# Conditioning's scale and shift on two engines, x normed on GpSimd and transposed early

## The chip, the cores and the metric

One Trainium2 chip, one of its cores. The metric is device time in microseconds of one execution of the whole program; the time before is the median of three runs, 3528.78 us.

## The reference

Two transformer blocks run one behind the other on x (512 tokens by 1024 features, float32), each with two layers of a mixer and a feed-forward part. What the change touches is the very beginning of the first block: a conditioning vector c gives a scale and a shift for each feature, x is normed over its features, scaled and shifted, and goes into the first projection of the first mixer.

```python
cond = jax.nn.silu(c)
mod = cond @ w_ada[layer] + b_ada[layer]            # 1024 -> 6 * 1024
sh1, sc1, g1, sh2, sc2, g2 = jnp.split(mod[:, None, :], 6, axis=-1)
h = rms_norm(x, norm_mix[layer]) * (1.0 + sc1) + sh1
proj = h @ w_in                                     # gated_deltanet_mixer, layer 0
```

## The kernel before

The program is written in Python loops that are fully unrolled; a planner then lays out each engine's queue by program order and by when it believes inputs to be ready, and each engine runs its queue in that order. Tiles are 128 partitions high. x lies in four tiles of 128 tokens by 1024 features, and the products want it turned: `h` is eight pairs of tiles (high part and low part, which together make up a float32) of 128 features by 512 tokens. Each product is three matmuls (`mm3`, lines 109 to 114): high by high, high weights by low h, low weights by high h. Weights come in through three raw buffers (`raw`), are split on ScalarE (line 88) and VectorE (line 89) into high and low parts, with three buffers each (`whi`, `wlo`).

`opening` (lines 179 to 208) works in two halves of four feature tiles, k0 = 0 and 4. Ahead of both, ScalarE squares x and sums it up by token; VectorE, then GpSimd (lines 84 and 85) make the inverse root `rs` for two token tiles at a time. For each half, the scale (i = 1) and then the shift (i = 0): two loads of 1 MB of `w_ada` (line 192), eight VectorE operations that multiply a slab of 128x512 by the conditioning's column and add it up into `acc` (lines 196 and 198), and `mod_cols` (lines 445 to 459), where four TensorE matmuls against a column of ones sum `acc` over partitions and VectorE adds the bias. In the first half four weight tiles are asked for next (`gdn_w_ab`, then the key, value and query tiles of head 0). `turned` (lines 141 to 166) norms x on VectorE into a raw buffer (line 146), transposes it on TensorE (line 151), applies scale and shift out of PSUM on VectorE (line 165) or ScalarE (line 163), and splits the result. Then come the products, bank by bank: four banks with four feature tiles each, 48 matmuls in each half, 96 in all. The banks' results are taken by `gdn`, which copies the first (line 545) and runs a convolution on each of the others (lines 602 and 603), and goes on with head 1's three projections.

Later in the program the same conditioning work is done in the background (`mod`, lines 423 to 443), one raw buffer at a time; its scale and shift go through `mod_cols` as well, eight matmuls each.

Of the kernel before, what the change touches and what calls it, by code (L numbers as in the profile page):

```python
# [9 lines left out]
F32 = mybir.dt.float32  # L10
F32R = mybir.dt.float32r
AF = mybir.ActivationFunctionType
ALU = mybir.AluOpType
# [3 lines left out]
P = 128  # L17
S = 512
D = 1024
NT = S // P  # L20
KD = D // P
# [9 lines left out]
class Net:  # L31
# [146 lines left out]

    def opening(self, pool, aps):

        nc = self.nc
        self.load_x()
        self.new_h()
        rs = [self.inverse_rms(u) for u in range(2)]
        ws, banks = [], [self.mm_bank() for _ in aps]
        for k0 in (0, 4):
            for i in (1, 0):
                n0 = i * D + k0 * P
                acc = pool.tile([P, 512], F32, name=self.nm("acc"))
                for c in range(2):  # L190
                    w = pool.tile([P, 4, 512], F32, name=self.nm("ada"))
                    nc.sync.dma_start(w, self.a["w_ada"][0, c * 512:(c + 1) * 512, n0:n0 + 512].rearrange("(k p) n -> p k n", p=P))
                    for k in range(4):
                        g = self.cond[:, 4 * c + k:4 * c + k + 1]
                        if c + k == 0:
                            nc.vector.tensor_scalar(acc, w[:, k, :], g, None, ALU.mult)
                        else:
                            nc.vector.scalar_tensor_tensor(acc, w[:, k, :], g, acc, ALU.mult, ALU.add)
                self.mod_cols(0, i, acc, k0, 4)
            if k0 == 0:  # L200
                ws = [self.weights(ap) for ap in aps]
            for u in range(2):
                self.turned(u, rs[u], k0, self.mods[0, 1], self.mods[0, 0])
            for (whi, wlo), bank in zip(ws, banks):
                for k in range(k0, k0 + 4):
                    s = slice(k * P, (k + 1) * P)
                    self.mm3(bank, (whi[:, s], wlo[:, s]), self.hk(k), k == 0, k == KD - 1)
        self.ready = banks
# [234 lines left out]
        return [lambda k=k: step(k) for k in range(KD)]  # L443

    def mod_cols(self, l, i, acc, j0, n):
        nc = self.nc
        if j0 == 0:
            self.mods[l, i] = self.mp.tile([P, KD], F32, tag=f"mod{i}", name=self.nm("mod"), bufs=2)
        o = self.mods[l, i][:, j0:j0 + n]
        b = self.mp.tile([P, KD], F32, tag="mb", name=self.nm("mb"), bufs=2)  # L450
        nc.sync.dma_start(b, self.a["b_ada_col"][l * 6 + i])
        pt = self.aux()
        for j in range(n):
            nc.tensor.matmul(pt[:, j:j + 1], acc[:, j * P:(j + 1) * P], self.ones[:, 0:1], start=True, stop=True)  # L454
        nc.vector.tensor_tensor(o, pt[:, :n], b[:, j0:j0 + n], ALU.add)
        if i % 3 == 1:
            g = self.mp.tile([P, KD], F32, tag="mg", name=self.nm("mg"), bufs=2)
            nc.sync.dma_start(g, self.a["norm_mix" if i == 1 else "norm_ffn"][l])
            nc.vector.scalar_tensor_tensor(o, o, 1.0, g[:, j0:j0 + n], ALU.add, ALU.mult)
# [1368 lines left out]
```

## Time and profile before

| | |
|---|---|
| runs | 3527.29, 3528.78, 3529.30 us; median 3528.78 |
| profiled execution | 3530.39 us; its span 3528.6 us |
| TensorE busy | 3444.9 us, 98% |
| VectorE busy | 2134.6 us, 60% |
| ScalarE busy | 1413.1 us, 40% |
| GpSimd busy | 175.0 us, 5% |

PE is TensorE's matmuls, PEld its weight loads, DVE is VectorE, ACT ScalarE, POOL GpSimd, SP the engine that issues the loads. The span runs from the first instruction of the profiled execution to its last, and times in the trace count from its start. Records of float32 matmuls come in pairs: one matmul of line 454 is two records. Matmuls are pipelined, so a record's duration is longer than the distance to the next record's start; the distance is what a matmul costs in a dense stretch.

### The profile page before, as it was taken

The numbers are of one execution on the slowest core, as the hardware profiler recorded it, in microseconds if no ns is written. First come the engines' busy times: TensorE is split into PE (matmuls) and PEld (weight loads), VectorE is DVE, ScalarE is ACT, GpSimd is POOL, SyncE is SP. The second block draws the span as 40 slices with busy tenths as digits, with TensorE's granted clock in tenths as the row PEclk, the third lists the DMA queues.
The fourth block names the chain that finished last, engine by engine and source line by source line (L and its number), as shares of the span: only waits on it lengthen the run. The fifth ranks groups of instructions, "written<-read, shape, count | busy, mean of one in ns | idle before, by whom it ended". The sixth has DMA issues, their size and how long they took to land.

```text
span 3528.6 us, 54339 instructions
## 1 busy us (share of the span) xinstructions
PE 3444.9 (98%) x21522; PEld 2992.9 (85%) x21522; DVE 2134.6 (60%) x3835; ACT 1413.1 (40%) x2867; POOL 175.0 (5%) x300
## 2 busy tenths in 40 slices
PE   6999999999999999999999999999999999999998
PEld 5888898989998889897777789898977778898988
DVE  7766675554455734349966645536489776456364
ACT  4444442223455422233445434434334544344342
POOL 0211100000211000000000000000000000000000
PEclk9999999999999999999999999999999999999999
DMA  6322145542332322244322232333353322233332
GB/s 218 96 90 78 41 140 188 185 147 87 110 103 78 118 93 95 93 150 138 93 84 73 72 119 92 94 99 99 115 159 90 96 70 72 83 119 101 97 97 78
DMA packets 137279, 374.68 MB, mean 106 GB/s; under 512 B 24480, under 2 KB 33392, under 8 KB 137024
## 3 DMA queue, kind: packets, MB, share of 16 engines
q1 hardware_dynamic: 137024, 371.20, 33.5%
q8 instruction: 170, 2.79, 0.3%
q14 instruction: 85, 0.70, 0.1%
HBM read 347.45 MB, written 8.48 MB: 101 GB/s over the span
## 4 chain that ended last, share of the span: by engine, by line
PE 89%; DVE 6%; ACT 2%; issue 1%; POOL 1%; DMA 0%; SPq 0%; DVEq 0%; POOLq 0%; ACTq 0%
PE mm L112 25%; PE mm L113 25%; PE mm L114 25%; PE aux L619 2%; PE mm L1459 2%; PE aux L1428 2%; DVE cy L1243 1%; PE aux L1450 1%; PE aux L608 1%; DVE wlo L89 1%; PE aux L151 1%; PE aux L952 1%; PE aux L454 1%; ACT aux L133 0%; PE mm L985 0%
## 5 line engine op out<-in xcount | busy, mean ns | idle before, releaser
L112 PE MATMUL mm<-hhi,whi 128*128 128x512 f32 (+1 forms) x2776 | 1057.5, 382 | 8.1 <-ACT hhi L88 6.4
L114 PE MATMUL mm<-hhi,wlo 128*128 128x512 f32 (+1 forms) x2776 | 1048.6, 378 | 4.1 <-DVE wlo L89 4.1
L113 PE MATMUL mm<-hlo,whi 128*128 128x512 f32 (+1 forms) x2776 | 1049.5, 379 | 0.0
L89 DVE TENSOR_TENSOR wlo<-raw,whi 128x1024 fp32r<-128x1024 f32 (+3 forms) x523 | 595.4, 1139 | 602.2 <-ACT whi L88 595.0
L88 ACT CAST whi<-raw 128x1024 fp32r<-128x1024 f32 (+3 forms) x523 | 512.7, 981 | 1046.0 <-PE mm L113 485.6
L112 PEld LDWEIGHTS mm<-hhi,whi 128*128 128x128 f32 x2776 | 524.5, 189 | 103.0 <-ACT hhi L88 7.2
L114 PEld LDWEIGHTS mm<-hhi,wlo 128*128 128x128 f32 x2776 | 524.8, 189 | 100.6 <-DVE wlo L89 5.2
L113 PEld LDWEIGHTS mm<-hlo,whi 128*128 128x128 f32 x2776 | 525.2, 189 | 93.3 <-issue 2.0
L112 PE MATMUL mm<-whi,hidhi 128*128 128x256 f32 x1056 | 297.2, 281 | 0.0
L114 PE MATMUL mm<-whi,hidlo 128*128 128x256 f32 x1056 | 297.1, 281 | 0.0
L113 PE MATMUL mm<-wlo,hidhi 128*128 128x256 f32 x1056 | 297.1, 281 | 0.0
L112 PE MATMUL mm<-whi,hhi 128*128 128x256 f32 (+1 forms) x736 | 216.0, 293 | 1.5 <-ACT whi L88 1.5
L114 PE MATMUL mm<-whi,hlo 128*128 128x256 f32 (+1 forms) x736 | 213.4, 290 | 0.0
L113 PE MATMUL mm<-wlo,hhi 128*128 128x256 f32 (+1 forms) x736 | 213.3, 290 | 0.0
L113 PEld LDWEIGHTS mm<-wlo,hidhi 128*128 128x128 f32 x1056 | 200.6, 190 | 0.3
L112 PEld LDWEIGHTS mm<-whi,hidhi 128*128 128x128 f32 x1056 | 200.6, 190 | 0.3
L114 PEld LDWEIGHTS mm<-whi,hidlo 128*128 128x128 f32 x1056 | 200.6, 190 | 0.0
L1243 DVE SCALAR_TENSOR_TENSOR cy<-cc,cw,cy 128x497 f32<-128x497 f32 (+19 forms) x240 | 177.0, 747 | 9.1 <-ACT cy L1240 5.3
L112 PEld LDWEIGHTS mm<-whi,hhi 128*128 128x128 f32 x736 | 140.8, 191 | 3.0 <-ACT whi L88 1.9
L113 PEld LDWEIGHTS mm<-wlo,hhi 128*128 128x128 f32 x736 | 140.8, 191 | 0.5 <-DVE wlo L89 0.2
L114 PEld LDWEIGHTS mm<-whi,hlo 128*128 128x128 f32 x736 | 140.8, 191 | 0.5 <-DVE hlo L89 0.2
L436 DVE SCALAR_TENSOR_TENSOR macc<-raw,cond,macc 128x1024 f32<-128x1024 f32 x70 | 89.8, 1283 | 76.9 <-DMA raw<-in_w_ada_dram 76.6
(383 smaller groups left out, 5261.1 us busy)
## 6 DMA issues: line engine op xcount, KB each, us to landing
raw<-in_w_ffn_in_dram SPq DMA_DIRECT2D x88, 512.0 KB, 3.6
raw<-in_ffn_w_up_dram SPq DMA_DIRECT2D x88, 512.0 KB, 3.6
raw<-in_w_ada_dram SPq DMA_DIRECT2D x80, 512.0 KB, 3.9
raw<-in_w_gate_dram SPq DMA_DIRECT2D x64, 512.0 KB, 3.6
raw<-in_w_in_dram SPq DMA_DIRECT2D x50, 512.0 KB, 3.5
raw<-in_gdn_w_in_dram SPq DMA_DIRECT2D x32, 512.0 KB, 3.8
raw<-in_w_ffn_out_dram SPq DMA_DIRECT2D x32, 512.0 KB, 3.6
raw<-in_w_branch_dram SPq DMA_DIRECT2D x64, 256.0 KB, 2.6
```

Source lines behind the costliest of these rows:

```text
L88: self.nc.scalar.copy(hi, src)
L89: self.nc.vector.tensor_tensor(lo, src, hi.bitcast(F32), ALU.subtract)
L112: mm(out, ahi, bhi, start=first, stop=False)
L113: mm(out, ahi, blo, start=False, stop=False)
L114: mm(out, alo, bhi, start=False, stop=last)
L151: nc.tensor.transpose(pt[:, i * 256 + v * P:i * 256 + (v + 1) * P], xn[:, v, (j + i) * P:(j + i + 1) * P], self.ident)
L436: nc.vector.scalar_tensor_tensor(acc[0], raw, self.cond[:, k:k + 1], acc[0], ALU.mult, ALU.add)
L454: nc.tensor.matmul(pt[:, j:j + 1], acc[:, j * P:(j + 1) * P], self.ones[:, 0:1], start=True, stop=True)
L619: T_.matmul(bank[:, sl[n]], l[:, sl[n]], r[:, sl[n]], start=True, stop=True)
L1243: taps.append(lambda d=d: stt(y[:, d:], c[:, :S - d], cw[:, f, 30 - d:31 - d], y[:, d:], ALU.mult, ALU.add))
L1428: T_.matmul(pt, qs[g][:, sl[i]], k[g][:, k0:k0 + w], start=b == 0, stop=b == 1)
L1459: T_.matmul(po[halves[g], sl[i]], v, p, start=b == 0 and coarse is not None, stop=last and b == len(todo) - 1)
```

## The change

In `opening` the loads of scale and shift of a half are issued one behind the other (`columns`). The scale is added up on VectorE as before. The shift is no longer: each of its eight 128x512 slabs becomes the stationary operand of four TensorE matmuls with the conditioning's column as the moving one, which accumulate in one PSUM bank; `mod_take`, split off from `mod_cols`, adds the bias. x is normed on GpSimd (`turn`) into buffers of its own, transposed, and copied by ScalarE to `xt`, ahead of scale and shift. These are then applied by feature tile over all 512 tokens: ScalarE makes the high part, VectorE the whole value in place and the low part. The fourth weight tile is split into buffers of its own. The products run feature tile by feature tile, the banks inside.

```diff
@@ -178,31 +178,65 @@
 
     def opening(self, pool, aps):
 
+
         nc = self.nc
         self.load_x()
         self.new_h()
         rs = [self.inverse_rms(u) for u in range(2)]
-        ws, banks = [], [self.mm_bank() for _ in aps]
+        banks = [self.mm_bank() for _ in aps]
+        xt = pool.tile([P, KD, S], F32, name="xt")
+
+        def columns(k0, i):
+
+            n0 = i * D + k0 * P
+            ws = []
+            for c in range(2):
+                w = pool.tile([P, 4, 512], F32, name=self.nm("ada"))
+                nc.sync.dma_start(w, self.a["w_ada"][0, c * 512:(c + 1) * 512, n0:n0 + 512].rearrange("(k p) n -> p k n", p=P))
+                ws += [w[:, k, :] for k in range(4)]
+            return ws
+
+        def turn(k0, u):
+            xn = pool.tile([P, 2, 512], F32, tag="xn", name=self.nm("xn"), bufs=2)
+            for v in range(2):
+                nc.gpsimd.tensor_scalar(xn[:, v, :], self.x[2 * u + v][:, k0 * P:(k0 + 4) * P], rs[u][:, v:v + 1], None, ALU.mult)
+            for j in (0, 2):
+                pt = self.aux()
+                for i in range(2):
+                    for v in range(2):
+                        nc.tensor.transpose(pt[:, i * 256 + v * P:i * 256 + (v + 1) * P],
+                                            xn[:, v, (j + i) * P:(j + i + 1) * P], self.ident)
+                nc.scalar.copy(xt[:, k0 + j:k0 + j + 2, u * 256:(u + 1) * 256], pt.rearrange("p (i c) -> p i c", i=2))
+
+        ws = []
         for k0 in (0, 4):
-            for i in (1, 0):
-                n0 = i * D + k0 * P
-                acc = pool.tile([P, 512], F32, name=self.nm("acc"))
-                for c in range(2):
-                    w = pool.tile([P, 4, 512], F32, name=self.nm("ada"))
-                    nc.sync.dma_start(w, self.a["w_ada"][0, c * 512:(c + 1) * 512, n0:n0 + 512].rearrange("(k p) n -> p k n", p=P))
-                    for k in range(4):
-                        g = self.cond[:, 4 * c + k:4 * c + k + 1]
-                        if c + k == 0:
-                            nc.vector.tensor_scalar(acc, w[:, k, :], g, None, ALU.mult)
-                        else:
-                            nc.vector.scalar_tensor_tensor(acc, w[:, k, :], g, acc, ALU.mult, ALU.add)
-                self.mod_cols(0, i, acc, k0, 4)
+            scale, shift = columns(k0, 1), columns(k0, 0)
+            acc = pool.tile([P, 512], F32, name=self.nm("acc"))
+            for k, w in enumerate(scale):
+                g = self.cond[:, k:k + 1]
+                if k == 0:
+                    nc.vector.tensor_scalar(acc, w, g, None, ALU.mult)
+                else:
+                    nc.vector.scalar_tensor_tensor(acc, w, g, acc, ALU.mult, ALU.add)
+            for u in range(2):
+                turn(k0, u)
+            self.mod_cols(0, 1, acc, k0, 4)
             if k0 == 0:
-                ws = [self.weights(ap) for ap in aps]
-            for u in range(2):
-                self.turned(u, rs[u], k0, self.mods[0, 1], self.mods[0, 0])
-            for (whi, wlo), bank in zip(ws, banks):
-                for k in range(k0, k0 + 4):
+                ws = [self.weights(ap, pool if i == 3 else None) for i, ap in enumerate(aps)]
+            pt = self.aux()
+            for k, w in enumerate(shift):
+                for j in range(4):
+                    nc.tensor.matmul(pt[:, j:j + 1], w[:, j * P:(j + 1) * P], self.cond[:, k:k + 1],
+                                     start=k + j == 0, stop=k == KD - 1 and j == 3)
+            self.mod_take(0, 0, pt, k0, 4)
+            gain, shift = self.mods[0, 1], self.mods[0, 0]
+            for k in range(k0, k0 + 4):
+                hi, lo = self.hk(k)
+                nc.scalar.activation(hi, xt[:, k, :], AF.Identity, bias=shift[:, k:k + 1], scale=gain[:, k:k + 1])
+                nc.vector.tensor_scalar(xt[:, k, :], xt[:, k, :], gain[:, k:k + 1], shift[:, k:k + 1], ALU.mult, ALU.add)
+                nc.vector.tensor_tensor(lo, xt[:, k, :], hi.bitcast(F32), ALU.subtract)
+            for k in range(k0, k0 + 4):
+                for (whi, wlo), bank in zip(ws, banks):
                     s = slice(k * P, (k + 1) * P)
                     self.mm3(bank, (whi[:, s], wlo[:, s]), self.hk(k), k == 0, k == KD - 1)
         self.ready = banks
@@ -443,15 +477,18 @@
         return [lambda k=k: step(k) for k in range(KD)]
 
     def mod_cols(self, l, i, acc, j0, n):
+        pt = self.aux()
+        for j in range(n):
+            self.nc.tensor.matmul(pt[:, j:j + 1], acc[:, j * P:(j + 1) * P], self.ones[:, 0:1], start=True, stop=True)
+        self.mod_take(l, i, pt, j0, n)
+
+    def mod_take(self, l, i, pt, j0, n):
         nc = self.nc
         if j0 == 0:
             self.mods[l, i] = self.mp.tile([P, KD], F32, tag=f"mod{i}", name=self.nm("mod"), bufs=2)
         o = self.mods[l, i][:, j0:j0 + n]
         b = self.mp.tile([P, KD], F32, tag="mb", name=self.nm("mb"), bufs=2)
         nc.sync.dma_start(b, self.a["b_ada_col"][l * 6 + i])
-        pt = self.aux()
-        for j in range(n):
-            nc.tensor.matmul(pt[:, j:j + 1], acc[:, j * P:(j + 1) * P], self.ones[:, 0:1], start=True, stop=True)
         nc.vector.tensor_tensor(o, pt[:, :n], b[:, j0:j0 + n], ALU.add)
         if i % 3 == 1:
             g = self.mp.tile([P, KD], F32, tag="mg", name=self.nm("mg"), bufs=2)
```

## Rows read from the trace of the kernel before

**Rows 1.** The page: busy time by engine; the chain that ended last, by engine.

```profile
PE 3444.9 (98%) x21522; PEld 2992.9 (85%) x21522; DVE 2134.6 (60%) x3835; ACT 1413.1 (40%) x2867; POOL 175.0 (5%) x300
...
PE 89%; DVE 6%; ACT 2%; issue 1%; POOL 1%; DMA 0%; SPq 0%; DVEq 0%; POOLq 0%; ACTq 0%
```

**Rows 2.** Table by stretch, opening: length, busy time by engine, clock, DMA.

```profile
11.80:38.30 26.50, 7.51 (x32) 6.81 (x32) 23.11 (x39) 6.13 (x11) 0.70 (x1) 1.00 0.92 350
...
49.30:55.80 6.50, 3.65 (x33) 3.40 (x31) 3.57 (x11) 3.08 (x8) 0.00 (x0) 1.00 0.40 101
```

**Rows 3.** Timeline of VectorE, opening: start, time, line, operation, count, idle before.

```profile
11.81 0.49 DVE L196 TENSOR_SCALAR acc<-ada,cond 128x512 f32<-128x512 f32 x1 [0.38 <-DMA ada<-in_w_ada_dram]
12.34 5.47 DVE L198 SCALAR_TENSOR_TENSOR acc<-ada,cond,acc 128x512 f32<-128x512 f32 x7
19.83 0.16 DVE L455 TENSOR_TENSOR mod<-aux,mb 128x4 f32<-128x4 f32 x1 [2.02 <-PE aux L454]
...
20.11 0.48 DVE L196 TENSOR_SCALAR acc<-ada,cond 128x512 f32<-128x512 f32 x1
...
30.41 1.67 DVE L146 TENSOR_SCALAR raw<-x,rs 128x512 f32<-128x512 f32 x4
```

**Rows 4.** Timeline of TensorE, opening.

```profile
17.96 1.83 PE L454 MATMUL aux<-ones,acc 128*128 128x1 f32 x8 [17.96 <-DVE acc L198]
...
31.00 3.81 PE L151 MATMUL aux<-ident,raw 128*128 128x128 f32 x16 [2.98 <-issue]
38.32 0.80 PE L112 MATMUL mm<-hhi,whi 128*128 128x512 f32 x1 [3.51 <-ACT hhi L88]
...
43.30 0.63 PE L114 MATMUL mm<-hhi,wlo 128*128 128x512 f32 x1
43.73 0.48 PE L112 MATMUL mm<-hhi,whi 128*128 128x512 f32 x1
...
49.30 1.84 PE L454 MATMUL aux<-ones,acc 128*128 128x1 f32 x16
51.00 1.95 PE L151 MATMUL aux<-ident,raw 128*128 128x128 f32 x16
55.81 0.73 PE L112 MATMUL mm<-hhi,whi 128*128 128x512 f32 x2 [2.86 <-ACT hhi L88]
...
69.61 0.39 PE L114 MATMUL mm<-hhi,wlo 128*128 128x512 f32 x1
```

**Rows 5.** Timeline of ScalarE, opening.

```profile
20.82 1.04 ACT L88 CAST whi<-raw 128x1024 fp32r<-128x1024 f32 x1 [9.57 <-DMA raw<-in_gdn_w_ab_dram]
```

**Rows 6.** Timeline of GpSimd, 0 to 140 us.

```profile
8.93 0.71 POOL L85 TENSOR_TENSOR rs<-rs,half 128x2 f32<-128x2 f32 x1
...
11.80 0.70 POOL L85 TENSOR_TENSOR rs<-rs,half 128x2 f32<-128x2 f32 x1
...
124.11 4.89 POOL L694 TENSOR_SCALAR tmp<-kn,dl 128x128 f32<-128x128 f32 x8
```

**Rows 7.** Timeline of VectorE, around 1590 us.

```profile
1587.62 4.00 DVE L1243 SCALAR_TENSOR_TENSOR cy<-cc,cw,cy 128x511 f32<-128x511 f32 x4 [0.88 <-ACT cy L1240]
...
1598.14 3.07 DVE L1243 SCALAR_TENSOR_TENSOR cy<-cc,cw,cy 128x505 f32<-128x505 f32 x4
```

**Rows 8.** Timeline of GpSimd, around 1580 us; line 1278 comes next at 1612.

```profile
1578.41 1.30 POOL L1278 TENSOR_TENSOR tmp<-tmp,sin 128x512 f32<-128x512 f32 x1 [25.00 <-DMA tmp<-tmp]
1588.08 1.42 POOL L1278 TENSOR_TENSOR tmp<-tmp,sin 128x512 f32<-128x512 f32 x1 [8.38 <-DMA tmp<-tmp]
```

**Rows 9.** Line 602 on ScalarE: shortest, median, longest ns; first and last start.

```profile
L602 ACT ACTIVATE cy<-mm,convw x24: 670/686/744, 64.6 to 367.1; 128x512 f32<-128x512 f32 x24
```

**Rows 10.** Table by stretch around 248 us; columns as in rows 2.

```profile
244.00:248.00 4.00, 2.27 (x14) 1.41 (x13) 1.97 (x7) 0.96 (x5) 2.79 (x6) 1.00 0.38 131
248.00:252.00 4.00, 4.00 (x20) 3.62 (x20) 1.77 (x5) 0.00 (x0) 0.00 (x0) 0.59 0.02 1
```

**Rows 11.** Timeline of TensorE around 248 us.

```profile
247.73 2.52 PE L454 MATMUL aux<-ones,macc 128*128 128x1 f32 x16
```

## Prediction

> **What bounds the kernel now.** I read the page first: TensorE is busy 98% of the span and holds 89% of the chain that ended last [rows 1]. So outside a few places time is TensorE's work, and an edit pays only where that engine is idle, or costs where it gets work. The table by stretch shows the opening as such a place [rows 2]: from 11.8 to 38.3 us TensorE is busy 7.5 us of 26.5, VectorE 23.1; from 49.3 to 55.8 there is a second hole.
>
> The VectorE timeline shows why [rows 3]. The first 1 MB of scale columns lands at 11.8, eight operations of 0.78 us add them up to 17.9, VectorE waits 2.0 us for four small matmuls (line 454), adds up the shift columns from 20.1, then norms x from 30.4. TensorE transposes at 31.0, and the first product starts at 38.3 [rows 4]. The products are 96: 36 up to 49.3 (bank 3's weights have no buffer yet), then 60, the last at 69.6, so the opening's products end at 69.8. From there TensorE is full; the change is worth what it does to that 69.8.
>
> Two more things stand in those rows. A 512-column product starts every 0.43 us up to 43.7 and every 0.23 after: 1.2 GHz, then 2.4, though the clock column reads 1.00 throughout. The 13 slow ones cost 13 x 0.20 = 2.6 us. And line 454's matmul with one column takes two records of 0.22 us at the low clock (8 in 1.8), 0.106 at the high (16 between 49.3 and 51.0).
>
> **Part by part.** *Loads.* Between the landing at 11.8 and w_ab's at 20.8 [rows 3, 5] come 3.5 MB in order, 2.6 us per MB: the shift columns land at 16.9 and 19.5. The change keeps that order on SP's queue; the two small loads that stood between move behind. Nothing here for the sum. The fourth weight tile now has its own split buffers but still waits for one of three raw buffers; its load is due long before the first product, so I give it nothing.
>
> *Shift on TensorE.* Gone: eight VectorE operations (6.2 us) and four matmuls for each half. New: 8 x 4 = 32 matmuls, 64 records, for each half: 64 x 0.22 = 14.2 us at the low clock, 6.8 at the high. In the first half nothing covers them: the engine has no products before the shift is there.
>
> *x normed on GpSimd.* Four VectorE operations (1.7 us) leave each half; eight GpSimd ones of 128x512 come in. No row has this operation at this size. Its bounds are the 128x128 one, 0.61 us [rows 6], and four times that, 2.4; I take 1.3, of a two-input operation of 128x512, the nearest shape [rows 8]. They need only x and the row scales, ready at 9.6 and 12.5 [rows 6], so GpSimd runs all eight at once (two buffers, freed by transposes), over VectorE's additions. These two disturb each other: four two-input VectorE operations took 4.00 us with one GpSimd operation beside them and 3.07 without [rows 7, 8], 0.9 us lost each. Two run before or at the start of the additions (0.4 us lost); with the other six the scale is added up at 17.9 + 0.4 + 6 x 0.95 = 24.0 instead of 17.9. At 0.61 us each (0.3 lost) it would be 20.1, at 2.4 (2.1 lost) 30.9.
>
> The Trainium skill (GPSIMD Engine Reference, section 3.1) puts a tight loop over 512 elements at 0.77 us; with that the loss is some 0.45 us each and the end 3 us earlier than I forecast, an estimate from that page. No row here shows it.
>
> *Order on TensorE.* In the kernel before, VectorE's queue has the first shift operation behind the scale's result (20.1 behind 19.8), though its columns had landed at 16.9 [rows 3]: the planner believes they come later than the scale is added up. I therefore expect the scale's four matmuls ahead of the shift's 32 in TensorE's queue, and the 64 records wait for the 24.0. Then 24.0 + 1.8 + 14.2 = 40.0. From a small matmul's end to the result on VectorE is 0.2 us [rows 3, 4], the ScalarE pass over 128x512 0.69 [rows 9], hand-overs 0.3: first product at 41.2, where it was 38.3. Transposing early saves the 3.8 us that stood ahead of the products, and is already in this; with the second half's last transposes in front as well it is up to 1.7 later.
>
> *Scale and shift by feature.* VectorE has two operations per feature tile (0.42 and at most 0.78) behind ScalarE's: 1.2 us against 12 products, 2.7 at the high clock, so only the first shows: some 0.5 us until the low part is there.
>
> *From the first product to the last.* 48 products at 0.228: 10.9; slow start 2.6; the second half's small matmuls, 72 records at 0.106: 7.7, between the products of the halves, as the planner has them now at 49.3 [rows 4]; hand-over 1.7; 48 products: 10.9; wait for the first low part 0.5. That is 34.3. Then the clock. At 247.7 a run of 16 such records took 2.5 us instead of 1.84, and the granted clock fell to 0.59 in it and stayed low past it [rows 10, 11]; ahead of it the engine had 1.7 us idle in 4. A run of 72 is four times as long, so I expect a fall in it: a third of the records at double price, 24 x 0.11 = 2.7 (0 if it doesn't fall, 7.7 if at once), and a slow start of the next products as at 38.3, 2.6. Sum 39.6: 41.2 + 39.6 = 80.8 against 69.8, **11.0 us later**. Below nothing I see no bound here: records that follow each other on one queue add.
>
> *Behind the opening.* Products now run feature by feature, so four banks end together at the end; before, the first convolution began at 64.6 [rows 9], 5.2 us ahead of it. VectorE gets these late. TensorE has three tiles of products for the next head meanwhile. I take 1 us, 0 to 4. In all **+12**: 3530.4 us, the profiled execution's time, becomes 3542.4; it lay 1.6 above the median of the runs, so 3541.
>
> **The rivals.** (1) *The shift's matmuls run ahead of the scale's.* If the planner sees them ready sooner, they start at 16.9: with transposes (1.9) and scale (1.8) 16.9 + 1.9 + 14.2 + 1.8 = 34.8, first product 36.0, end 75.6: +5.8 and 1, 3536. For it: columns land ahead of 24.0. Against: the order in rows 3.
>
> (2) *The small matmuls raise the clock, and the change is not slower.* Place: the 64 records ahead of the first product. Price: half of what remains after the rise. In rows 4 the clock rose 5.4 us after work became dense. From 24.0 on: 24 records slow, 48 at 0.106 = 5.1, shift at 34.5, first product 35.7, no slow starts, no fall: 35.7 + 0.5 + 10.9 + 7.7 + 1.7 + 10.9 = 67.4, 2.4 us earlier: with the 1 us behind it 3527. It decides from a rise before about 32 us. Combined with (1), it is 16.9 + 5.4 + 56 x 0.106 = 28.2, first product 29.4, end 61.1: 3521, the only way to clearly faster that I see. Against both: rows 10 and 11, where such a run did not hold the clock up.
>
> The Trainium skill (TensorE: Matmul & The Clock Gate, Part 1) says that activity of the engine releases the throttle, with no word on one-column matmuls. Taken literally it gives rival 2, 3527; rows 10 and 11 speak against that reading and no row settles it.
>
> (3) *GpSimd at the upper bound*, 2.4 us each: additions end 6.9 us later still, 3548; with the backlog at 4 us, 3551.
>
> **How the numbers follow.** Forecast 0.55 (3537 to 3546 within it); rival 1 0.16; rival 2 alone 0.13; 1 and 2 together 0.07; rival 3 0.09. A difference of 0.2%, 7 us, is what a measurement of this kernel can tell from none: faster is below 3521.7, slower above 3535.8. Faster: 0.06, of the combined rival. Same: rival 2, half of rival 1, the rest of the combined one and a forecast without the second fall: 0.25. Slower: 0.69. Range 3526 to 3550.
>
> **What would show it.** On VectorE: the eighth addition of the scale ends near 24 instead of 17.9, with GpSimd operations of 1.3 us between. On TensorE: 72 records of 0.22 us from 24 to 40 with no faster ones; first product near 41; between the halves some 12 us without products, with records turning from 0.11 to 0.22; last product near 81. I am wrong if records of the first run come every 0.11 us, if they start at 17, or if GpSimd leaves the additions alone; and on the end if TensorE waits for VectorE after it.

## The result, and the profile after

| | before | after |
|---|---|---|
| median of the runs beside each other | 3528.53 us (3527.29 to 3529.30) | 3551.51 us (3547.75 to 3553.47) |
| ratio after to before, 95% interval | | 1.0066 [1.0052, 1.0080] |
| profiled execution; its span | 3530.39; 3528.6 us | 3550.76; 3549.0 us |
| first product of the opening starts | 38.3 us | 43.2 us |
| last one ends | 70.0 us | 81.4 us |
| from there to the end of the span | 3458.6 us | 3467.6 us |

The change is slower, by 23.0 us in the medians and 20.4 in the profiled executions. Of these 20.4, the opening itself holds 11.4 (81.4 against 70.0), where 11.0 had been forecast; what comes behind it holds 9.0, where 1 had been. The direction was right, the size was not: 3551.5 lies above the 3550 at which the range ended. Of the kernels in the experiments below, e4, e7, e15 and e16 had one run each of 4109 to 10508 us, which their medians leave out.

The page, busy time by engine and the chain by engine, beside [rows 1]:

```profile
PE 3467.4 (98%) x21634; PEld 3013.0 (85%) x21634; DVE 2120.9 (60%) x3803; ACT 1412.0 (40%) x2859; POOL 190.9 (5%) x308
...
PE 79%; DVE 4%; ACT 2%; issue 1%; POOL 0%; DVEq 0%; POOLq 0%; ACTq 0%
```

TensorE has 112 records more (2 x 64 for the shift, 16 gone) and 22.5 us more busy time; VectorE has lost 13.7. The page alone looks like "TensorE works longer, and that is all". The timelines tell more. TensorE in the opening, to hold against [rows 4]:

```profile
22.23 1.84 PE L482 MATMUL aux<-ones,acc 128*128 128x1 f32 x8
23.93 6.96 PE L229 MATMUL aux<-cond,ada 128*128 128x1 f32 x32
30.75 3.38 PE L207 MATMUL aux<-ident,xn 128*128 128x128 f32 x14
33.92 3.83 PE L229 MATMUL aux<-cond,ada 128*128 128x1 f32 x32
37.62 0.56 PE L207 MATMUL aux<-ident,xn 128*128 128x128 f32 x2
43.17 1.65 PE L112 MATMUL mm<-hhi,whi 128*128 128x512 f32 x3 [4.99 <-ACT hhi L235]
...
57.57 10.10 PE L229 MATMUL aux<-cond,ada 128*128 128x1 f32 x64
68.83 1.65 PE L112 MATMUL mm<-hhi,whi 128*128 128x512 f32 x3 [1.16 <-ACT hhi L235]
...
81.03 0.39 PE L114 MATMUL mm<-hhi,tlo 128*128 128x512 f32 x1
```

Line 229 is the shift, 482 the scale's sum over partitions, 207 the transposes. The shift's 64 records stand alone on the engine, in both halves, as forecast. Two things were not: the second half's transposes cut into them (30.75), and 5 us pass between the end of the records and the first product. Why the scale comes when it does, VectorE, ScalarE and GpSimd tell (beside [rows 3] and [rows 6]):

```profile
15.04 0.16 DVE L137 TENSOR_REDUCE rs<-sq 128x2 f32<-128x4 f32 x1 [6.52 <-ACT aux L133]
15.12 0.49 DVE L218 TENSOR_SCALAR acc<-ada,cond 128x512 f32<-128x512 f32 x1
15.64 6.44 DVE L220 SCALAR_TENSOR_TENSOR acc<-ada,cond,acc 128x512 f32<-128x512 f32 x7
24.10 0.16 DVE L492 TENSOR_TENSOR mod<-aux,mb 128x4 f32<-128x4 f32 x1 [2.02 <-PE aux L482]
...
13.80 0.58 ACT L209 COPY xt<-aux 128x512 f32<-128x512 f32 x1 [3.35 <-PE aux L207]
14.28 0.61 ACT L133 ACTIVATE aux<-x 128x512 f32<-128x512 f32 x1
...
9.69 3.11 POOL L202 TENSOR_SCALAR xn<-x,rs 128x512 f32<-128x512 f32 x2
17.08 9.95 POOL L202 TENSOR_SCALAR xn<-x,rs 128x512 f32<-128x512 f32 x6
```

Read from below: GpSimd's first two norm operations take 1.56 us each, transposes follow, and ScalarE has the copy of the transposed x (13.80, after 3.35 us of waiting) in its queue ahead of the eighth square (14.28). The reduction of the squares on VectorE waits for that square, and the scale's additions stand behind the reduction: they begin at 15.1, not at 11.8.

The wait ahead of the first product, on ScalarE and VectorE:

```profile
38.21 0.58 ACT L209 COPY xt<-aux 128x512 f32<-128x512 f32 x1 [3.89 <-PE aux L207]
38.69 2.94 ACT L88 CAST whi<-raw 128x1024 fp32r<-128x1024 f32 x3
42.30 2.93 ACT L235 ACTIVATE hhi<-xt,mod,mod 128x512 fp32r<-128x512 f32 x4 [0.67 <-DVE mod L492]
...
39.77 2.36 DVE L89 TENSOR_TENSOR wlo<-raw,whi 128x1024 fp32r<-128x1024 f32 x2 [15.15 <-ACT whi L88]
42.05 0.15 DVE L492 TENSOR_TENSOR mod<-aux,mb 128x4 f32<-128x4 f32 x1
```

The shift's sums are done at 37.75, but the bias is added to them at 42.05: that operation stands on VectorE behind two weight splits, these wait for casts, and the casts stand on ScalarE behind a copy whose transposes TensorE ran after the shift (37.62). VectorE has been idle for 15 us.

Behind the opening, by stretch (columns as in [rows 2]); the first row is the 60 us that begin with the next product of the kernel before, the second the same of the kernel after:

```profile
70.28:130.28 60.00, 59.62 (x368) 51.66 (x367) 51.78 (x102) 31.27 (x78) 13.55 (x24) 1.00 0.38 122
82.57:142.57 60.00, 54.41 (x320) 47.01 (x319) 51.72 (x103) 30.04 (x76) 10.64 (x19) 0.94 0.40 126
104.00:116.00 12.00, 9.28 (x59) 7.65 (x58) 11.91 (x33) 7.21 (x20) 3.17 (x8) 1.00 0.13 44
116.00:128.00 12.00, 11.19 (x69) 10.63 (x70) 9.64 (x14) 3.84 (x6) 0.00 (x0) 0.72 0.41 132
```

TensorE idles 5.6 us where it idled 0.4, and the granted clock falls to 0.72 behind the stretch with the longest gap, in which VectorE was full (11.9 of 12). That gap, followed back over TensorE, ScalarE, the loads' queue and VectorE:

```profile
115.02 0.50 PE L112 MATMUL mm<-hhi,whi 128*128 128x512 f32 x1 [2.48 <-ACT whi L88]
...
113.93 1.04 ACT L88 CAST whi<-raw 128x1024 fp32r<-128x1024 f32 x1
...
110.25 0.33 SPq L103 DMA_DIRECT2D raw<-in_gdn_w_in_dram  x1
...
108.95 1.27 DVE L470 SCALAR_TENSOR_TENSOR macc<-raw,cond,macc 128x1024 f32<-128x1024 f32 x1
```

A background step of the conditioning held one of the three raw buffers until VectorE, late with four banks' convolutions at once, came to it (108.95 to 110.22). At 110.25 the next weight was asked for; it landed, was cast at 113.9, and TensorE had run out of products. Another 1.1 us behind this gap and 1.4 us at 89.7 were spent waiting for VectorE directly.

Does this make up the 9.0? A longer stretch with equal work tells: from the end of the opening to the first operation of `add_gated` behind the mixer (at 456.90 before and 477.57 after). TensorE has the same records in it in every kernel here. The rows are before, after, and e3 and e17 from the experiments:

```profile
70.00:456.90 386.90, 379.84 (x2767) 331.17 (x2768) 275.91 (x512) 178.76 (x464) 67.25 (x128) 0.98 0.26 82
81.42:477.57 396.15, 382.52 (x2767) 332.62 (x2768) 278.73 (x518) 181.75 (x469) 70.41 (x128) 0.98 0.26 82
85.71:472.53 386.82, 375.90 (x2768) 327.41 (x2768) 277.55 (x515) 182.54 (x469) 66.72 (x128) 1.00 0.27 84
85.68:475.90 390.22, 378.51 (x2768) 326.83 (x2768) 280.43 (x519) 180.97 (x469) 69.86 (x128) 1.00 0.28 86
```

The change loses 9.3 us in it, 6.6 of them idle and 2.7 in slower records; behind it the two kernels take the same time, 3071.7 and 3071.4 us. So the whole loss lies there. The 60 us above hold 5.2 us of that idle time and the 12 us at a granted clock of 0.72. A caution for all that follows: behind that point all kernels run the same source lines, and yet their single profiled executions took 3065.7 to 3074.1 us there.

### The profile page after: what moved, and what is told of

It is laid out like the page before. It is cut to its first block, busy times and chain, and to the rows that moved or that the text cites. A ratio compares the mean times of both kernels' runs of the same rounds, so it can differ in the third digit from the quotient of the medians.

```text
span 3549.0 us, 54531 instructions
## 1 busy us (share of the span) xinstructions
PE 3467.4 (98%) x21634; PEld 3013.0 (85%) x21634; DVE 2120.9 (60%) x3803; ACT 1412.0 (40%) x2859; POOL 190.9 (5%) x308
## 4 chain that ended last, share of the span: by engine, by line
PE 79%; DVE 4%; ACT 2%; issue 1%; POOL 0%; DVEq 0%; POOLq 0%; ACTq 0%
PE mm L112 23%; PE mm L114 23%; PE mm L113 23%; PE mm L1496 2%; PE aux L1465 2%; PE aux L1487 1%; DVE cy L1280 1%; PE aux L151 1%; DVE wlo L89 1%; PE aux L989 1%; ACT aux L133 0%; PE mm L1022 0%; PE aux L1012 0%; PE aux L1417 0%; POOL rs L85 0%
## 5 line engine op out<-in xcount | busy, mean ns | idle before, releaser
L89 DVE TENSOR_TENSOR wlo<-raw,whi 128x1024 fp32r<-128x1024 f32 (+2 forms) x522 | 594.0, 1139 | 612.4 <-ACT whi L88 604.6
L88 ACT CAST whi<-raw 128x1024 fp32r<-128x1024 f32 (+2 forms) x522 | 511.4, 980 | 1043.4 <-PE mm L113 488.3
```

The lines of the kernel that those rows point to most:

```text
L88: self.nc.scalar.copy(hi, src)
L89: self.nc.vector.tensor_tensor(lo, src, hi.bitcast(F32), ALU.subtract)
```

## The experiments

All times are medians, the ratio against runs of the kernel before on the same chip. The groups of experiments ran on different chips, with medians of 3527.9 to 3529.6 us for the kernel before, so small differences between groups are better read from the ratios. "First" is the start of the first product, "end" the end of the opening's last, both in the profiled execution; "idle" is TensorE's idle time in the 60 us that begin with the next product. The diffs below are cut to the lines that matter; `...` stands for what is left out.

| kernel | us | ratio [95%] | first | end | idle |
|---|---|---|---|---|---|
| before | 3528.5 | | 38.3 | 70.0 | 0.4 |
| after | 3551.5 | 1.0066 [1.0052, 1.0080] | 43.2 | 81.4 | 5.6 |
| e1 shift on VectorE | 3536.1 | 1.0020 [1.0010, 1.0029] | 35.1 | 69.0 | 3.0 |
| e2 norm on VectorE | 3554.0 | 1.0075 [1.0062, 1.0088] | 46.1 | 85.3 | 5.9 |
| e3 banks one by one | 3542.6 | 1.0040 [1.0026, 1.0053] | 46.3 | 85.7 | 1.5 |
| e4 other space | 3551.3 | 1.0070 [1.0056, 1.0083] | 46.2 | 88.6 | 6.8 |
| e5 = e1 + e3 | 3532.5 | 1.0014 [1.0005, 1.0023] | 35.2 | 69.4 | 2.7 |
| e6 = e1 + e2 + e3 | 3530.6 | 1.0008 [0.9999, 1.0017] | 33.9 | 67.5 | 3.0 |
| e7 before, by feature | 3536.0 | 1.0027 [1.0016, 1.0038] | 39.6 | 71.3 | 1.8 |
| e8 wide shift | 3537.6 | 1.0029 [1.0017, 1.0040] | 35.7 | 71.0 | 1.3 |
| e10 = e8 + e3 | 3537.9 | 1.0027 [1.0016, 1.0037] | 35.9 | 71.1 | 1.8 |
| e11 second turn late | 3549.8 | 1.0057 [1.0043, 1.0070] | 40.7 | 82.8 | 6.5 |
| e12 wide, then VectorE | 3531.6 | 1.0007 [0.9998, 1.0015] | 36.8 | 69.4 | 2.4 |
| e13 = e3 + e4 | 3549.1 | 1.0059 [1.0047, 1.0071] | 42.9 | 81.3 | 5.6 |
| e14 = e10 + e4 | 3541.3 | 1.0035 [1.0023, 1.0047] | 36.8 | 72.4 | 4.4 |
| e15 = e6 + e4 | 3526.5 | 0.9995 [0.9986, 1.0004] | 33.8 | 69.6 | 0.1 |
| e16 = e12 + e4 | 3533.4 | 1.0017 [1.0009, 1.0026] | 37.2 | 70.1 | 0.8 |
| e17 background held off | 3548.9 | 1.0050 [1.0037, 1.0064] | 46.3 | 85.7 | 1.4 |
| e18 = e15, held off | 3532.1 | 1.0007 [0.9998, 1.0015] | 33.8 | 68.8 | 0.7 |

**e1: the shift back on VectorE.**

```diff
-                    nc.tensor.matmul(pt[:, j:j + 1], w[:, j * P:(j + 1) * P], self.cond[:, k:k + 1], ...)
-            self.mod_take(0, 0, pt, k0, 4)
 ...
+                    nc.vector.scalar_tensor_tensor(acc, w, g, acc, ALU.mult, ALU.add)
+            self.mod_cols(0, 0, acc, k0, 4)
```

> The changed kernel with the shift added up on VectorE again, as the scale is; all else as changed. Theory (the cost is the shift's one-column matmuls on TensorE): the first 64 records go, VectorE adds the shift up from 22 to 29 instead, so the first product comes at 33 to 36 us instead of 43.2; between the halves the 72 records of 11 us become 16 of about 1.8, the clock does not fall there. Sum 16 to 20 us back: 3531 to 3536. Rival (GpSimd beside VectorE's additions is the cost): the additions of the shift suffer as well, at most 5 us back, 3546 or more. Rival (what is lost behind the opening, some 9 us, grows or falls by itself): the opening's last product comes as much earlier as the theory says, but the time does not follow it by more than 3 us.

15.4 us come back, two thirds of the loss. The opening now ends 1.0 us ahead of the kernel before, yet the time stays 7.9 above it: something behind the opening is lost without the shift's records too (393.5 us in the stretch of equal work, for 386.9).

**e2: the norm back on VectorE.**

```diff
-                nc.gpsimd.tensor_scalar(xn[:, v, :], ...)
+                nc.vector.tensor_scalar(xn[:, v, :], ...)
```

> The changed kernel with x normed on VectorE instead of GpSimd; all else as changed. Theory (the shift's records on TensorE are the cost, GpSimd only delays their start): scale added up at 18 to 20 us instead of 22.1, the rest moves with it: 2 to 4 us back, 3547 to 3550. Rival (GpSimd beside VectorE is the cost): 8 us or more back, 3543 or less.

Nothing comes back, the intervals overlap. The scale's four matmuls start at 22.1 as with GpSimd: the norm's own operations stand ahead of the additions and between them instead. So e2 puts one delay in the place of another, and the disturbance by GpSimd, a main term of my sum, can't be read from it; the profile after shows it, 1.0 us (below).

**e3: products bank by bank, and e4: the fourth weight's split buffers in space that lives on.**

```diff
-            for k in range(k0, k0 + 4):
-                for (whi, wlo), bank in zip(ws, banks):
+            for (whi, wlo), bank in zip(ws, banks):
+                for k in range(k0, k0 + 4):
```

```diff
-                ws = [self.weights(ap, pool if i == 3 else None) for i, ap in enumerate(aps)]
+                ws = [self.weights(ap, self.mp if i == 3 else None) for i, ap in enumerate(aps)]
```

> The changed kernel with the products bank by bank again inside each half, as before the change. Theory (behind the opening 9 us are lost because four banks end together, so that their copies and convolutions all come late): the last product stays at 81, and 4 to 9 us come back: 3542 to 3547. Rival (they are lost because the small loads of the next stage wait for the opening's space): no more than 2 us back, 3549 to 3552.

> The changed kernel with the fourth weight tile's two split buffers in a pool that outlives the opening, so that the next stage's first loads don't wait for the last product that reads them. Theory (banks end together): loads start earlier, but no more than 2 us come back, 3549 to 3552. Rival (the loads' wait is the loss): the first convolution starts earlier, 4 to 9 us come back: 3542 to 3547.

e3 gives 8.9 us back though its opening ends 4.3 us later; idle behind it is 1.5 instead of 5.6, and the stretch of equal work takes 386.8 us, as in the kernel before. e4 gives nothing. In e3's profile the clock did not rise in the shift's records, which is 3.0 of the 4.3 us:

```profile
33.96 6.83 PE L229 MATMUL aux<-cond,ada 128*128 128x1 f32 x32
40.65 0.67 PE L207 MATMUL aux<-ident,xn 128*128 128x128 f32 x2
46.31 1.22 PE L112 MATMUL mm<-hhi,whi 128*128 128x512 f32 x2 [5.00 <-ACT hhi L235]
...
86.86:146.86 60.00, 58.51 (x343) 50.18 (x342) 54.95 (x107) 31.54 (x78) 7.39 (x14) 1.00 0.43 136
```

The same 32 records took 3.83 us in the profile of the changed kernel and in e13, 6.83 in e3, e4 and e17: some 3 us by the clock's luck, so the ends of single profiles are compared with that in mind.

**e5, e6: the two losses together.**

> The changed kernel with two parts undone at once: the shift added up on VectorE again, and the products bank by bank. Alone, the first gave 15.4 us back and the second 8.9. Theory (two losses at two places: the shift's 64 records per half ahead of the products, and four banks that end together behind them): both add, 3551.5 - 15.4 - 8.9 = 3527, with the opening's last product near 68.8 as with the first alone and the next head's products near 457, as in the kernel before, where they start at 457.4. Rival (the loss behind is VectorE being late because the shift's result is late, and the bank order pays only by covering that): they do not add, 3534 to 3536, no better than the first part alone.

> As the kernel with shift on VectorE and products bank by bank, and with x normed on VectorE too; what remains of the change is x transposed ahead of scale and shift, these applied by feature, and the loads side by side. Theory (GpSimd's norm costs VectorE about what the norm costs VectorE itself, as norming on VectorE alone moved the time from 3551.5 to 3554.0): 3527 to 3530, level with the kernel before. Rival (with the shift on VectorE too, VectorE is the bound of the opening, and 8 more operations of 0.42 us put the first product 3.4 us later): 3531 and more. Other rival (transposing early saves the 3.8 us that stood ahead of the products): 3523.

They add only in part: 3532.5 where 3527 was expected; with the opening ending near 70 the order is worth 3.6 us or nothing (the intervals of e1 and e5 overlap), not 8.9. With the norm on VectorE too the time is level with the kernel before, and its opening, 2.5 us earlier, does not show in it.

**e7: the kernel before, by feature.** The order of e3's diff reversed in the kernel before, and the fourth weight split into the opening's space.

> The kernel before with one thing of the change: the products of the opening run feature tile by feature tile, banks inside (and the fourth weight tile split into buffers of its own, without which its products would hold up the others). Conditioning, norm and transposes as before. Theory (four banks that end together are the loss behind the opening, wherever the opening ends): 3528.2 + 8 to 9 = 3536 to 3537, with the last product of the opening near 69.8 as before, TensorE idle some 5 us between 70 and 120 and the granted clock below 1.00 there. Rival (the loss behind needs the late opening, with ScalarE and VectorE behind on other work): 3528 to 3530.

The time is as expected, 3536.0. But its profiled execution (3532.3 us) is the lowest of its runs, and shows 1.8 us idle behind the opening, not 5; the end of the opening accounts for 1.3, the stretch of equal work for 3.1 (390.0 us). Order and space were not told apart here.

**e8: the shift by wide records.**

```diff
-                    nc.tensor.matmul(pt[:, j:j + 1], w[:, j * P:(j + 1) * P], self.cond[:, k:k + 1], ...)
+                nc.tensor.matmul(row[0:1, :], self.cond[:, k:k + 1], w, start=k == 0, stop=k == KD - 1)
+            nc.scalar.copy(line[0:1, :], row[0:1, :])
 ...
+                nc.tensor.matmul(pt[:, j:j + 1], line[0:1, j * P:(j + 1) * P], self.ones[0:1, 0:1], start=True, stop=True)
```

> The changed kernel with the shift still on TensorE, by other records: the conditioning's column is the stationary operand and the 128x512 slab the moving one, 8 matmuls of 512 columns into one row for each half instead of 32 of one column; ScalarE copies the row out and four small matmuls turn it into columns. The columns that TensorE streams for the shift go from 32 to 4096, the records from 64 to 16 and 8. Theory (it is the many records with little in them that make the shift dear and let the clock fall): granted clock 1.00 from 40 to 80 us where it was 0.80 and 0.74, 48 products in 10.9 us where they took 12.2, the shift of the second half in 5 to 7 us where its records took 10.1; about 3540. Rival (the clock goes by what came before, idle time, and a full pass over float32 columns costs as much): shift 8 to 14 us in either half, 3550 or above.

14 us come back with the shift still on TensorE (13 by the ratios). Its TensorE, ScalarE, and a stretch of its second shift:

```profile
23.93 3.49 PE L228 MATMUL aux<-ada,cond 128*1 128x512 f32 x4
27.25 5.31 PE L228 MATMUL aux<-ada,cond 128*1 128x512 f32 x12
33.23 1.05 PE L233 MATMUL aux<-ones,line 1*128 1x1 f32 x8 [0.67 <-ACT line L230]
34.21 1.75 PE L207 MATMUL aux<-ident,xn 128*128 128x128 f32 x14
35.72 0.94 PE L112 MATMUL mm<-hhi,whi 128*128 128x512 f32 x3
...
22.57 1.99 ACT L88 CAST whi<-raw 128x1024 fp32r<-128x1024 f32 x2
...
48.50:55.70 7.20, 7.11 (x18) 1.32 (x17) 0.99 (x3) 0.06 (x1) 0.00 (x0) 1.00 0.25 75
```

The clock stays up in the second shift (1.00), as expected; over 40 to 80 us it was 0.95 and 0.97, not 1.00. In the first shift it rose within the run: the first four records fill 3.3 us, 0.83 us each, the other twelve start 0.43 us apart, though the clock column reads 1.00 for both. But the shift is not much cheaper: 10.4 us from its start to its columns, where the narrow records took 10.8 in the profile after, half of them after the clock's rise; and 8.7 us in the second half, where 5 to 7 was expected. What is gone is the order: the casts run at 22.6, the transposes behind the shift, the first product follows 1.4 us behind it instead of 5.4.

**e10: wide, bank by bank.** e3's diff on e8.

> The kernel with the shift by 512-column matmuls on TensorE (3537.6), and the products bank by bank as well: of the change it keeps the shift on TensorE and the norm on GpSimd. Theory (the feature order is a loss of its own behind the opening, 8.9 us with the kernel as changed): opening ends near 70.6 as with the wide shift alone, time 3528 to 3530, level with the kernel before. Rival (bank order pays in full only behind a late opening; behind one that ends near 70 it gave 3.6 us, from 3536.1 to 3532.5 with the shift on VectorE): 3534.

The order gives nothing here; both expectations were too good. In these runs it pays beyond doubt behind a late opening only.

**e11: the second half's turn late.** Shift by narrow records, as in the change.

```diff
+            if k0 == 0:
+                late = [pool.tile([P, 2], F32, name=self.nm("late")) for _ in rs]
+                for a, b in zip(late, rs):
+                    nc.vector.scalar_tensor_tensor(a, shift[:, 0:2], 0.0, b, ALU.mult, ALU.add)
+                rs = late
```

> The changed kernel, the second half's row scales made again on VectorE behind the first half's shift (two operations on 128x2, rs + 0 x shift), so that the second half's norm and transposes can't be queued ahead of the first half's products; nothing else differs, shift by 64 records of one column. Theory (part of the late first product is order in the queues: transposes among the shift's records, the weights' casts on ScalarE behind the last copy of transposed x, the shift's addition on VectorE behind the splits that wait for these casts): records run without a break from 24.0 to 38, casts end before 30, result of the shift 0.3 us behind the last record, then 0.4 for the row scales, 1.6 for the first GpSimd operation and a transpose that stands ahead of the first product: 40.5, where it was 43.2 in the profile of the changed kernel and 46.1 to 46.3 in two with the same front. Time 3546 to 3548. Rival (the delay is in the small matmuls' own results, not in the queues): first product at 43 or later, 3551.

```profile
23.64 13.79 PE L229 MATMUL aux<-cond,ada 128*128 128x1 f32 x64
40.59 0.47 PE L207 MATMUL aux<-ident,xn 128*128 128x128 f32 x1 [3.16 <-POOL xn L202]
40.72 1.63 PE L112 MATMUL mm<-hhi,whi 128*128 128x512 f32 x3
...
22.66 2.94 ACT L88 CAST whi<-raw 128x1024 fp32r<-128x1024 f32 x3
37.73 2.93 ACT L240 ACTIVATE hhi<-xt,mod,mod 128x512 fp32r<-128x512 f32 x4 [12.12 <-DVE mod L497]
```

The queues do what the theory says: casts at 22.7, the pass over x 0.3 us behind the last record instead of 4.5. The first product, at 40.7, stands behind a transpose that waits for the norm made late. The time is 1.8 us better by the medians and 3.2 by the ratios, with overlapping intervals, where 3.5 to 5.5 was expected: the transposes that were pushed back now stand between the halves, and the opening ends at 82.8. So order in the queues is the cause of the 5 us ahead of the first product, but those 5 us are not worth 5.

**e12: wide shift in the first half, VectorE in the second.** e8's diff in the first half, e1's in the second, e3's in both.

> As the wide shift with products bank by bank, but the wide shift in the first half alone; in the second half the shift is added up on VectorE. In the first half VectorE is late with the scale and TensorE has room; in the second TensorE has 11.0 us between the products of the halves, 9 of them for the shift's matmuls, while VectorE waits. Theory: first product near 35.7, scale and shift of the second half added up by 41.1 + 12.5 = 53.6, two more us to the first product of the second half, 55.6 instead of 58.5, the opening ends near 67.7, and the time is 3 us below that of the kernel with the wide shift in both halves and bank order. Rival (what the opening gains by ending before 70 is waited for behind it, as with scale, shift and norm all on VectorE, where it ended at 67.1 and the time was 3530.6): no gain on that kernel.

The first products of both halves come 1 us later than expected (36.8 and 56.7) and the opening ends 1.7 later, yet the time is 6.3 us below e10, where 3 was expected, and level with the kernel before.

**e13 to e16: order and space together.** e4's diff on e3, e10, e6 and e12.

> The changed kernel with products bank by bank and the fourth weight's split buffers in space that lives on, so that the opening's space, in which the next stage's small tables and the copy of the first bank come to lie, is free some 10 us ahead of the last product. Alone, the order gave 8.9 us (3542.6) and the space nothing (3553.0, with the banks ending together). Theory (order and space bind each other: the first bank's copy comes early only if both its products and its space are done): the copy moves from 0.5 us behind the last product to 4 to 6 us ahead of it, TensorE idles 1 us or less in the 60 us behind the opening instead of 1.5, time 3538 to 3540. Rival (the order does it alone): 3542 to 3543.

> The wide shift with products bank by bank (3537.9, where the order gave nothing) and the fourth weight's split buffers in space that lives on. Theory (space held to the last product is why the order gave nothing there): first bank's copy 4 to 6 us ahead of the end of the opening, which stays near 70.6; TensorE idle in the 60 us behind it 1 us instead of 2.5; time 3534 to 3535, and 3530 if the 5.1 us of idle from 130 to 300 us goes as well (3.1 in the kernel before). Rival: 3538.

> Scale, shift and norm on VectorE with products bank by bank (3530.6, opening's end 67.1 against 70.3 before, yet no faster), and the fourth weight's split buffers in space that lives on. Theory (what the opening gained was lost to the space held to its end: 3.7 us of idle behind it, among it 2.9 for a product behind tables that were loaded after the last product): idle 1 us, time 3526 to 3528, at or under the kernel before (3528). Rival: 3530 to 3531.

> Wide shift in the first half, VectorE in the second, bank by bank (3531.6), and the fourth weight's split buffers in space that lives on. Theory: idle behind the opening 1 us instead of 2.4, 3529 to 3530. Rival: 3531 to 3532.

In all four the copy of the first bank moved ahead of the opening's end, as expected. The time followed in e15 alone: 4.0 us less than e6, TensorE idle 0.1 us, the best version, and by its interval level with the kernel before. e13, e14 and e16 came out 2 to 7 us slower than their partners. The intervals overlap in each pair, so none of these differences is sure, but a gain of 3 to 5 us in all four is excluded by the three that went the other way. In e13 and e14 a wait for a weight's cast (2.7 and 2.1 us) takes the place of the one removed, by the same chain as at 115.02 in the change: the load was asked for within 0.1 us of the end of VectorE's background step (at 108.8 and 99.9), here with the banks one by one. The theory that order and space bind each other falls as a rule for all of them.

**e17, e18: the background held off.** On the change, and on e15 as a control.

```diff
-        if self.background:
+        self.asked = getattr(self, "asked", 0) + 1
+        if self.background and self.asked > 12:
             self.background.pop(0)()
```

> The changed kernel with the background conditioning started 8 steps later: the first 12 weights ask for no step of it, so that for some 70 us behind the opening the three raw buffers are the weights' alone; the 8 steps follow at the end of the stage. The opening is left as it is (last product at 81 to 89 by the clock's luck). Theory (behind the opening VectorE has four banks' convolutions at once; a background step stands in its queue to 110.2 us and holds a raw buffer, the next weight is asked for at 110.25, cast at 113.9, and TensorE waits 2.5 us for it and 1.1 after it, with the granted clock at 0.72 beyond): weights land early, that wait is gone, TensorE idle in the 60 us behind the opening 2 us or less instead of 5.6, clock there 1.00; 3551.5 - 3.6 - 3 = 3545. Rival (VectorE's convolutions themselves are what is waited for): idle as before, 3550 or more.

> The same 8 steps held off in the version that came out nearest to the kernel before (scale, shift and norm on VectorE, bank by bank, own space; 3526.5). There TensorE idles only 0.06 us in the 60 us behind the opening, so by the theory nothing is to be gained there: 3525 to 3528. If it comes out at 3522 or less, the background's share of VectorE and of the buffers costs elsewhere too.

```profile
87.33:147.33 60.00, 58.59 (x355) 50.52 (x354) 49.79 (x103) 31.45 (x78) 10.56 (x21) 1.00 0.34 107
```

Idle time and clock came as expected, 1.4 us and 1.00, and from the opening's end to the end of the span the profiled execution took 3461.7 us instead of 3467.6, 5.9 less where 6.6 was expected. The median fell by 2.7 only, to 3548.9 where 3545 was expected; against the kernel before on the same chip the ratio fell from 1.0066 to 1.0050, which is 5.6 us, with overlapping intervals. Two reasons for a smaller gain stand in the runs: the opening's end at 85.7 (the shift's records at the low clock, 6.83 us), and the control, which lost 5.5 us by the medians and 4.2 by the ratios, again with overlapping intervals, where nothing was to be had (388.8 us in the stretch of equal work, for 383.5 in e15): steps held off cost elsewhere. That these two make up the difference is worked out, not shown.

## Why the prediction was right or wrong

**What bounds the kernel: right, and too narrow.** The opening moved as forecast, to 0.4 us, and that is luck in part: the shift's sums were ready 2.2 us earlier than forecast (37.75 for 40.0), the hand-over cost 4.2 more, the stretch from the first product to the last 1.4 less. "From there TensorE is full" held for the kernel before alone.

**GpSimd and the scale: the end near, the working wrong.** Forecast end of the additions 24.0, measured 22.1. GpSimd's operations took 1.56 us alone and 1.57 to 1.90 beside the additions, 1.3 was taken. Three of the six ran beside the additions, and each made one of these longer by some 0.33 us, as here:

```profile
17.21 1.10 DVE L220 SCALAR_TENSOR_TENSOR acc<-ada,cond,acc 128x512 f32<-128x512 f32 x1
18.34 0.75 DVE L220 SCALAR_TENSOR_TENSOR acc<-ada,cond,acc 128x512 f32<-128x512 f32 x1
```

That is 1.0 us lost, not 5.7 by six operations: the row I sized this by [rows 7] overstated it. In its place came 3.3 us that were in no term: the additions began at 15.1, behind a reduction that waits for the eighth square, behind a copy of transposed x. "Transposing early saves the 3.8 us" left out what the moved step's copies are queued ahead of. The Trainium skill (GPSIMD Engine Reference, section 3.1) gives 0.77 us as the best case of a tight loop over 512 elements; this operation is not near it in the trace, with 1.56 us and more.

**Order on TensorE: right.** Scale at 22.2, shift at 23.9, records of 0.22 us: 13.8 for 64 where the clock stayed low (e11), as the 14.2 said. In the profile after it rose behind the 14 transposes that cut into them (33.92). So rival 2 came true for half of the first run of records, and won 3.0 us there; the queues behind it took 4.2 more than the 1.2 of the forecast.

**The hand-over, 1.2 us: wrong, 5.4.** The moved transposes' copy on ScalarE is ahead of the casts, these are ahead of the splits, these ahead of the shift's bias on VectorE; e11 shows it. First product at 43.2, and 46.3 where the clock did not rise, for 41.2.

**From the first product to the last: right.** 38.2 us for 39.6. The clock did fall in the second run of records: granted 0.97 up to 62.0, 0.50 from there to 68.8, the 64 records in 10.1 us where 6.8 + 2.7 = 9.5 was taken, and products started slow behind it.

```profile
56.70:62.00 5.30, 5.30 (x49) 5.26 (x47) 0.32 (x2) 0.00 (x0) 0.00 (x0) 0.97 0.04 11
62.00:68.80 6.80, 5.67 (x27) 5.58 (x27) 0.16 (x1) 0.83 (x2) 0.00 (x0) 0.50 0.01 2
```

**Behind the opening, 1 us with 0 to 4: wrong, 9.0.** This is the step that failed, with 8.0 of the 8.4 us by which the profiled execution missed its forecast (3550.8 for 3542.4); the prediction's own sign for it, TensorE waiting for VectorE behind the opening, came. I counted that four banks now end together, and covered it with three tiles of the next head's products. The cover needs weights, the weights need raw buffers, and one of these was in the hands of VectorE, the engine I had just called late. Banks one by one (e3: idle 1.5, 8.9 us less) and the background held off (e17: idle 1.4; 5.9 us less in the stretch of equal work) each take the wait away from the changed kernel. What stays open is what the wait becomes in other arrangements: order and space moved times by 2 to 7 us in either direction (e13 to e16), and I could not forecast them. Of these the stretch of equal work shows two: e13 lost 5.8 us in it to e3, e15 gained 6.0 on e6. In e14 and e16 it was 0.4 and 2.0 us shorter than in their partners although the medians rose; why they rose is not shown.

**Rivals.** Rival 1 did not happen. Rival 3's 3551 is the time that came, by another way: its GpSimd price of 2.4 us was 1.66, and its backlog of 4 us was 9.

## What to carry to other kernels

Moving a step earlier moves all its instructions ahead in every queue it uses: ask of each one what stands behind it, above all where the moved step's input comes later than that of its new neighbours. When producers are made to finish together, follow the cover's own supply (weights, their buffers, who frees these) to the engine that the change makes late. A term "behind it" deserves the same walk over queues as the stage itself; here it was sized from one row and was 9 us, not 1. And between two forms of the same work, ask which of them lets the clock rise: e8's wide records did, the narrow ones of the same price did not.

## What was not expected of the hardware

The clock's rise was not the same behind the same front: 32 one-column records behind 14 transposes took 3.83 us in two profiles (after, e13) and 6.83 in three others (e3, e4, e17), of kernels whose TensorE queues are alike up to there. By the distance of the records that is the 2.4 GHz level and the 1.2 GHz level; the granted clock's column reads 1.00 in both. One-column records alone never brought it up: 64 of them ran 13.8 us at the low level in e11. The Trainium skill (TensorE: Matmul & The Clock Gate, Part 1) has activity release the throttle; these records, back to back, did not.

Records of 512 columns into one row did bring it up, in all five kernels that have them, within the first run: in e8 from 0.83 us a record to 0.43. So eight wide matmuls did in 8.6 us what 32 narrow ones did in 13.8, and nearly all of the difference is the clock. At one and the same level they cost the same: at the high one 2 x 0.43 = 0.86 us for a wide one and 8 x 0.11 = 0.88 for the four narrow ones (eight records) that it replaces, at the low one 2 x 0.83 = 1.66 and 8 x 0.215 = 1.72.
